# A convolution with max pooling on one core: three row combinations, two loads and the last stores change places

## The chip, the core and the metric

The kernel runs on one core of one Trainium2 chip. Each of the core's engines works through its own list of instructions in order and waits for the others through semaphores: TensorE (PE in the profile) multiplies matrices into PSUM, VectorE (DVE), ScalarE (ACT) and GpSimd (POOL) do elementwise work, and SyncE (SP) issues most of the transfers. GpSimd and ScalarE issue a few transfers too. The metric is the device time of one execution in microseconds. Three runs of the kernel before took 104.82, 105.14 and 105.29 us, so its median is 105.14 us.

## What is computed

```python
# x: 16 images, 64 channels, 64 x 64, fp32;  weight: 128 x 64 x 3 x 3, fp32;  pool_size = 2
x_pad = np.pad(x, ((0, 0), (0, 0), (1, 1), (1, 1)))
conv[b, co] = sum over ci, kh, kw of weight[co, ci, kh, kw] * x_pad[b, ci, kh:kh+64, kw:kw+64]
output[b, co, i, j] = max of conv[b, co, 2*i:2*i+2, 2*j:2*j+2]     # 16 x 128 x 32 x 32
```

## The kernel before

**Tiles.** Two images share the 128 partitions: 64 input channels of the first (half 0) and 64 of the second (half 1). A unit is one quarter of an image pair: 16 rows of the convolution, which after pooling are 8 rows of output. There are 32 units of two kinds, 13 of kind K and 19 of kind W, in the sequence given by `SEQ` (L37). Every matmul uses 64 of the 128 partitions, so a matmul of half 0 and one of half 1 run side by side on PE. The order writes them as pairs, such as `P2.1.0+PBa.1.1`; the first number is the unit, the second the half. A product is three matmuls (the three columns of the 3 x 3 weights), and a pair of products takes PE 0.65 us.

**Fewer products per unit.** For each pair of convolution rows that are pooled together, the kernel does not compute two rows with three weight rows each. It combines input rows (and weight rows) first:

- A W unit has four row combinations, each 128 x 512 and cast to bf16, in `row_op` (L254): `E` or `e` (an odd minus an even row, on VectorE or GpSimd), `S` (their sum, on VectorE), `Z` and `Y` (differences, on GpSimd). Four products use them: `P2` uses E, `P0` uses Z, `P3` uses Y, `P1` uses S.
- A K unit reads a bf16 copy of the input rows for its products `PAa`, `PAb`, `PBa` and `PBb`, and has one row sum, `KS` (VectorE), for its fifth product `PR`.

**From PSUM to the output.** Each unit and half has an even-row bank `ta` and an odd-row bank `tb`, of eight PSUM banks in all. ScalarE copies the even bank to SBUF (`EV`, `ev`: L290). VectorE takes the larger of the even and odd rows, in place (`MX`, `mx`: L299). The product `P1` or `PR` is added after that. ScalarE then copies the odd columns (`OD`, `od`: L303), VectorE takes the larger of the columns (`CM`, `cm`: L327), which frees the bank, and a transfer stores the unit. For a W unit ScalarE also fills the odd bank with the negated even bank (`SE`: L295), once P2 stands there. Capitals before a dot and a number are steps of K units for EV, MX, OD and CM, and small letters those of W units.

**What sets the order.** One list, `ORDER` (L425), gives the order in which instructions are emitted, and with it the order on every engine. Two kinds of waits are added by hand:

- `on_gpsimd` (L81) makes a GpSimd row combination wait for the last VectorE instruction emitted so far that was marked with `on_vector` (the KS, S and E row combinations, and the early weight work and casts).
- `behind` (L73) makes a load wait for a named instruction, kept in `mark`. The input of the W units comes in four chunks for each image pair (`LD.0` to `LD.3` for the first pair, `wload`, L107). LD.1 waits for GM, LD.2 for E.0 and LD.3 for E.1 (L375). All of them are issued by SyncE, which also issues the stores, in order. The input of the K units comes through GpSimd (`L0`, `L1` and so on, `kload`, L101), which issues them in its own order between row combinations.

**The last stores.** The last two units, K 12 and W 18, are stored half by half. `act_left` counts the ScalarE steps that are still to be emitted. While more than one is left, a half is stored by SyncE at once. After that the store is kept in `late` and emitted when no ScalarE step is left, by ScalarE and SyncE in turn.

Of the kernel before, what the change touches and what calls it, by code (L numbers as in the profile page):

```python
# [10 lines left out]
def kernel(  # L11
# [8 lines left out]
    nc = tc.nc  # L20
# [24 lines left out]
    for c in SEQ.lower():  # L45
        i = sum(1 for g in place if g[0] == c)
# [19 lines left out]
    acc = psum.tile([128, 8, R, W], FP32, name="acc")  # L66
# [6 lines left out]
    def behind(inst, other):  # L73
        if other is not None:
            tc.add_manual_dep(inst.ins, other.ins.name, SYNC, reason="order")
# [9 lines left out]
    def rows_of(p, lo, hi):  # L85
        return x[2 * p : 2 * p + 2].rearrange("b c h w -> (b c) h w")[:, lo:hi, :]

    def chunk(q):
        return (2 * R * q + (q > 0), min(H, 2 * R * (q + 1) + 1))
# [17 lines left out]
    def wload(i):  # L107
        loaded.add(i)
        p, q = place["w", i]
        lo, hi = chunk(q)  # L110
        if i % NQ == 0 and q:
            lo -= 2
        return nc.sync.dma_start(
            out=wx[i // NQ % 3][:, lo + 1 : hi + 1, :], in_=rows_of(p, lo, hi)
        )
# [17 lines left out]
    D2, G0, D0, G2, GM, G1, GP = range(1, 29, 4)  # L133
# [48 lines left out]
    ta, tb = {}, {}  # L182
# [69 lines left out]
    mark = {}  # L252
# [33 lines left out]
    ev, od, ot = {}, {}, {}  # L286

    def evac(*g):
        ev[g] = ev_pool.tile([128, R, W], FP32, name="ev")
        nc.scalar.copy(out=ev[g], in_=acc[:, ta[g]])  # L290
        free.add(ta.pop(g))

    def seed(i, h, bank):
# [12 lines left out]
    act_left = [0]  # L306
# [2 lines left out]

    def store_late(dst, src):  # L310
        late.append((dst, src))
        if act_left[0] <= 1:
            flush_late()

    def flush_late():
        while late and act_left[0] == 0:
            stored["late"] = stored.get("late", 0) + 1
            queue = nc.scalar if stored["late"] % 2 else nc.sync
            dst, src = late.pop(0)
            queue.dma_start(out=dst, in_=src)  # L320

    def colmax(c, i, h):
        g = (c, i, h)
        if (c, i) not in ot:
            ot[c, i] = o_pool.tile([128, 2, R, WO], FP32, name="o")
        o = ot[c, i]
        nc.vector.tensor_tensor(  # L327
            out=o[:, h],
            in0=acc[:, tb[g], :, 0::2],
            in1=od.pop(g),  # L330
            op=MAX,
        )
        free.add(tb.pop(g))
        p, q = place[c, i]
        dst = out[2 * p : 2 * p + 2, :, q * R : (q + 1) * R, :].rearrange("b c h w -> c b (h w)")
        src = o.rearrange("p b h w -> p b (h w)")
        stored[c, i] = stored.get((c, i), 0) + 1
        if order_of.index((c, i)) >= len(order_of) - 2:
            if act_left[0] <= 1:
                store_late(dst[:, h], src[:, h])  # L340
            else:
                nc.sync.dma_start(out=dst[:, h], in_=src[:, h])
        elif stored[c, i] == 2:
            nc.sync.dma_start(out=dst, in_=src)
# [27 lines left out]
        return made[0]  # L372

    def load_w(i):
        behind(wload(i), mark.get({0: "D2", 1: "GM", 2: "E0", 3: "E1"}.get(i)))  # L375

    def note(name, inst):
        mark[name] = inst
# [4 lines left out]
    def load_k(n):  # L383
# [22 lines left out]
        "X2": lambda e: cast_more(e, 1, khi2 - klo2),  # L406
        "KX2": lambda: behind(load_second(), mark["D2"]),
        "LD": load_w,
        "L": load_k,
        "KS": lambda i: note(f"KS{i}", ks(i)), "S": ws, "Z": wz, "Y": wy, "SE": seed,  # L410
# [6 lines left out]
    for name, f in ("ev", evac), ("mx", rowmax), ("od", odd), ("cm", colmax):  # L417
        steps[name] = lambda i, h, f=f: f("w", i, h)
        steps[name.upper()] = lambda i, h, f=f: f("k", i, h)
# [4 lines left out]

    ORDER = """  # L425
        D0/V g2 g1/P D2 g0 TD0:1 GS/V TD2:4 KX2 XO1/A TG1:0 VD2/V TG0:2 GP/V XO/A TG2:3 VG0/A
        PAx.0.0:6+PAx.0.1:7 GM/V PAa.0.0+PAa.0.1 VD0/A VG1/V LD.1 PAb.0.0+PAb.0.1 XE/V VG2/A TGM:2 KS.0
        TGP:4 E.0 VGM/A PBa.0.0:0+PBa.0.1:1 EV.0.0 Z.0 VGP/V LD.2 PBb.0.0+PBb.0.1 EV.0.1 MX.0.0
        P2.0.0:4+P2.0.1:3 X1/A S.0 X1b/A L0 PAy.1.0:7+PAy.1.1:2 PAa.1.0+PAa.1.1 SE.0.1:5 MX.0.1 Y.0 SE.0.0:6
        PAb.1.0+PAb.1.1 X2/A E.1 PR.0.0+P0.0.1 EV.1.0 P0.0.0+PR.0.1 EV.1.1 S.1 LD.3 ev.0.1 PBa.1.0:7+P3.0.1 KS.1 Z.1 OD.0.1  # L430
        P2.1.0:2+PBa.1.1:3 OD.0.0 CM.0.1 ev.0.0 mx.0.1 P3.0.0+PBb.1.1 SE.1.0:4 Y.1 PBb.1.0+P2.1.1:1 MX.1.1
        P0.1.0+P1.0.1 CM.0.0 e.2 MX.1.0 SE.1.1:0 P3.1.0+PR.1.1 LD.4 mx.0.0 ev.1.0 PR.1.0+P0.1.1 Y.2 LD.5
        OD.1.1 mx.1.0 od.0.1 P1.0.0+P3.1.1 OD.1.0 CM.1.1 ev.1.1 P1.1.0+P2.2.1:2 cm.0.1 Z.2 od.0.0 mx.1.1
        PAa.2.0:5+PAa.2.1:3 SE.2.1:1 CM.1.0 PAb.2.0+PAb.2.1 L1 od.1.0 cm.0.0 KS.3 PBa.2.0:7+PBa.2.1:6 EV.2.1
        E.3 LD.6 PBb.2.0+P0.2.1 EV.2.0 S.2 LD.7 P2.2.0:3+P1.1.1 KS.2 ev.2.1 Z.3 cm.1.0 PAa.3.0:5+PBb.2.1
# [62 lines left out]
    for s in ORDER.split():  # L498
        act_left[0] -= on_act(s)
        if s[0] == "P":  # L500
            made = []
            for p in s.split("+"):
                p, _, bank = p.partition(":")
                n, i, h = p.split(".")
# [48 lines left out]
```

## Time and profile before

| | |
|---|---|
| Median of 3 runs | 105.14 us |
| The profiled execution, its own time | 105.48 us |
| its span, first to last instruction | 103.6 us |
| PE busy | 97.3 us (94%), 894 matmuls |
| DVE busy | 89.2 us (86%) |
| ACT busy | 81.9 us (79%) |
| POOL busy | 67.1 us (65%) |
| Granted PE clock | 0.995 of full speed |
| DMA moved | 22.81 MB, 220 GB/s on average |

Positions in the text, such as "at 12.50", are microseconds from the start of the span. The profiled execution spends 1.9 us outside its span. PE works with hardly a pause from 16.77 to the end of its list, so what is lost or won before that point shows at the end if the other engines keep up. In the first 17 us PE, DVE and POOL wait for each other and for transfers in turn.

### The profile page before, as it was taken

The numbers are of one execution on the slowest core, as the hardware profiler recorded it, in microseconds if no ns is written. First come the engines' busy times: TensorE is split into PE (matmuls) and PEld (weight loads), VectorE is DVE, ScalarE is ACT, GpSimd is POOL, SyncE is SP. The second block draws the span as 40 slices with busy tenths as digits, with TensorE's granted clock in tenths as the row PEclk, the third lists the DMA queues.
The fourth block names the chain that finished last, engine by engine and source line by source line (L and its number), as shares of the span: only waits on it lengthen the run. The fifth ranks groups of instructions, "written<-read, shape, count | busy, mean of one in ns | idle before, by whom it ended". The sixth has DMA issues, their size and how long they took to land.

```text
span 103.6 us, 2522 instructions
## 1 busy us (share of the span) xinstructions
PE 97.3 (94%) x894; PEld 53.4 (52%) x894; DVE 89.2 (86%) x178; ACT 81.9 (79%) x178; POOL 67.1 (65%) x76
## 2 busy tenths in 40 slices
PE   6899998999999999999999999999999999999920
PEld 2365434555665555555555755555555555666600
DVE  1697598999698999987988999989999999989960
ACT  4579966887897867799879988889889988988640
POOL 7306559947959687976895946892993598590000
PEclk9999999999999999999999999999999999999997
DMA  2987988899999997589989988999956841512352
GB/s 59 354 284 224 234 196 286 237 300 165 284 382 320 161 212 291 192 201 206 218 195 327 357 224 264 299 218 222 378 190 139 197 173 41 196 70 76 131 210 96
DMA packets 13069, 22.81 MB, mean 220 GB/s; under 512 B 1024, under 2 KB 9216, under 8 KB 13056
## 3 DMA queue, kind: packets, MB, share of 16 engines
q1 hardware_dynamic: 12048, 19.63, 58.0%
q0 software_dynamic: 864, 2.88, 18.8%
q8 instruction: 7, 0.11, 0.5%
q10 hardware_dynamic: 144, 0.13, 0.4%
q14 instruction: 6, 0.05, 0.2%
HBM read 17.14 MB, written 8.39 MB: 246 GB/s over the span
## 4 chain that ended last, share of the span: by engine, by line
PE 76%; DMA 8%; DVE 8%; POOL 2%; issue 2%
PE acc L202 75%; DMA wx<-in_x_dram 6%; DMA wraw<-in_weight_dram 3%; DVE acc L299 2%; DVE o L327 2%; POOL wz L260 1%; POOL wy L260 1%; DVE wq L395 1%; DVE we L260 1%; DVE ws L260 1%; DVE wq L364 0%; DVE wq L356 0%; DVE wt L180 0%; PE acc L164 0%; DVE ks L260 0%
## 5 line engine op out<-in xcount | busy, mean ns | idle before, releaser
L202 PEld LDWEIGHTS <-wt 64*128 64x128 bf16 x858 | 50.8, 94 | 41.3 <-issue 1.2
L202 PE MATMUL acc<-kx,wt 64*128 64x512 bf16 (+4 forms) x324 | 57.1, 365 | 0.0
L299 DVE TENSOR_TENSOR acc<-acc,ev 128x512 f32<-128x512 f32 x64 | 42.4, 692 | 4.1 <-PE acc L202 2.5
L290 ACT COPY ev<-acc 128x512 f32<-128x512 f32 x64 | 36.6, 592 | 6.2 <-PE acc L202 5.7
L260 POOL TENSOR_TENSOR wz<-wx 128x512 bf16<-128x512 f32 x19 | 24.1, 1273 | 10.9 <-DVE ks L260 4.6
L202 PE MATMUL acc<-wy,wt 64*128 64x504 bf16 (+1 forms) x114 | 29.6, 377 | 0.4 <-POOL wy L260 0.4
L260 POOL TENSOR_TENSOR wy<-wx 128x512 bf16<-128x512 f32 x19 | 24.1, 1272 | 8.2 <-PE acc L202 3.1
L202 PE MATMUL acc<-wz,wt 64*128 64x504 bf16 (+1 forms) x114 | 29.2, 376 | 0.2 <-POOL wz L260 0.2
L202 PE MATMUL acc<-we,wt 64*128 64x504 bf16 (+1 forms) x114 | 29.1, 377 | 0.0
L202 PE MATMUL acc<-ws,wt 64*128 64x504 bf16 (+1 forms) x114 | 29.1, 377 | 0.0
L327 DVE TENSOR_TENSOR o<-acc,od 128x256 f32<-128x256 f32 x64 | 25.2, 417 | 2.1 <-ACT od L303 1.7
L303 ACT COPY od<-acc 128x256 f32<-128x256 f32 x64 | 23.0, 380 | 4.5 <-PE acc L202 3.7
L295 ACT ACTIVATE acc<-acc 128x512 f32<-128x512 f32 x38 | 22.1, 587 | 3.8 <-DVE o L327 2.1
L202 PE MATMUL acc<-ks,wt 64*128 64x504 bf16 (+1 forms) x78 | 20.2, 377 | 0.0
L260 POOL TENSOR_TENSOR we<-wx 128x512 bf16<-128x512 f32 x11 | 14.0, 1272 | 5.1 <-PE acc L202 3.4
L260 DVE TENSOR_TENSOR ws<-wx 128x512 bf16<-128x512 f32 x19 | 13.9, 738 | 0.0
L260 DVE TENSOR_TENSOR we<-wx 128x512 bf16<-128x512 f32 x8 | 6.0, 750 | 1.1 <-DMA wx<-in_x_dram 1.1
L260 DVE TENSOR_TENSOR ks<-kx 128x512 bf16<-128x512 bf16 x13 | 5.4, 419 | 0.1
L105 POOL DMA_DIRECT2D kx<-in_x_dram x6 | 3.5, 590 | 0.0
L487 PE MATMUL acc<-const-bfloat16-1.0 128*128 128x512 bf16 x6 | 2.7, 623 | 0.8 <-PEq L534 0.8
L356 DVE TENSOR_TENSOR wq<-wraw 128x192 bf16<-128x192 f32 x1 | 0.5, 502 | 2.4 <-DMA wraw<-in_weight_dram 2.4
L164 PE MATMUL acc<-ident,wq 128*128 128x128 bf16 x28 | 2.1, 220 | 0.5 <-DVE wq L395 0.3
(28 smaller groups left out, 17.6 us busy)
## 6 DMA issues: line engine op xcount, KB each, us to landing
out_dram<-o SPq DMA_DIRECT2D x30, 256.0 KB, 4.6
wx<-in_x_dram SPq DMA_DIRECT2D x9, 512.0 KB, 7.1
wx<-in_x_dram SPq DMA_DIRECT2D x5, 480.0 KB, 6.4
wx<-in_x_dram SPq DMA_DIRECT2D x4, 544.0 KB, 6.4
kx<-in_x_dram POOLq DMA_DIRECT2D x3, 496.0 KB, 8.0
kx<-in_x_dram POOLq DMA_DIRECT2D x2, 528.0 KB, 8.9
wx<-in_x_dram SPq DMA_DIRECT2D x1, 576.0 KB, 9.9
ksecond<-in_x_dram SPq DMA_DIRECT2D x2, 256.0 KB, 4.1
```

The costliest lines, as they stand in the source:

```text
L105: return nc.gpsimd.dma_start(out=ktile(i)[:, lo:hi, :], in_=rows_of(p, lo, hi))
L164: nc.tensor.transpose(turned_rows(m)[:, j, :], wq[:, BLOCKS[m] - 1 + j : BLOCKS[m] + 1 + j, :].rearrange("a b c -> a (b c)"), ident,)
L202: lambda kw=kw, o0=o0, o1=o1, c0=c0, c1=c1: nc.tensor.matmul(dst[:, i0:i1, o0:o1], wt[lo : lo + CI, m0 + kw - h, :], rows(lo, i0, i1, c0, c1),
L260: return engine.tensor_tensor(out=r, in0=t[:, f + a : f + a + 2 * R - 1 : 2, :], in1=t[:, f + b : f + b + 2 * R - 1 : 2, :], op=op,)
L290: nc.scalar.copy(out=ev[g], in_=acc[:, ta[g]])
L295: nc.scalar.mul(acc[:, t], acc[:, ta["w", i, h]], -1.0)
L299: nc.vector.tensor_tensor(out=t, in0=t, in1=ev.pop(g), op=MAX)
L303: nc.scalar.copy(out=od[g], in_=acc[:, tb[g], :, 1::2])
L327: nc.vector.tensor_tensor(out=o[:, h], in0=acc[:, tb[g], :, 0::2], in1=od.pop(g), op=MAX,)
L356: inst = engine.tensor_tensor(out=slots(D0), in0=g0, in1=g1, op=SUB)
L395: "D2", on_vector(nc.vector.tensor_sub(out=slots(D2), in0=g2, in1=g1))
L487: warm = nc.tensor.matmul(acc[:, n], src[:, 0:128], src, start=True, stop=True, skip_group_check=True)
```

## The change

- LD.2, the third chunk, is emitted right behind KS.0 and waits for KS.0 where it waited for E.0. The order of SyncE's list stays the same.
- LD.3, the fourth chunk, is emitted behind CM.0.1 and waits for it, where it waited for E.1.
- S.1 leaves its place behind E.1 and is emitted behind MX.1.0, ahead of e.2. KS.1 and Z.1 are emitted directly behind E.1.
- Because `on_gpsimd` looks at the last marked VectorE instruction, e.2 now waits for S.1. It waited for KS.1 before. Z.1 waits for KS.1 as it did.
- The limit for keeping a store in `late` goes from one ScalarE step left to two. So the store of half 0 of W 18 (cm.18.0) is kept as well, and the last three stores go by ScalarE, SyncE and ScalarE. Before, cm.18.0 went by SyncE at once, CM.12.0 by ScalarE and cm.18.1 by SyncE.
- `mark["EV"]` is written and never read.

```diff
     def evac(*g):
         ev[g] = ev_pool.tile([128, R, W], FP32, name="ev")
-        nc.scalar.copy(out=ev[g], in_=acc[:, ta[g]])
+        mark["EV"] = nc.scalar.copy(out=ev[g], in_=acc[:, ta[g]])
...
     def store_late(dst, src):
         late.append((dst, src))
-        if act_left[0] <= 1:
-            flush_late()
+        flush_late()
...
         o = ot[c, i]
-        nc.vector.tensor_tensor(
+        mark["CM"] = nc.vector.tensor_tensor(
             out=o[:, h],
...
-            if act_left[0] <= 1:
+            if act_left[0] <= 2:
                 store_late(dst[:, h], src[:, h])
...
     def load_w(i):
-        behind(wload(i), mark.get({0: "D2", 1: "GM", 2: "E0", 3: "E1"}.get(i)))
+        behind(wload(i), mark.get({0: "D2", 1: "GM", 2: "KS0", 3: "CM"}.get(i)))
...
-        PAx.0.0:6+PAx.0.1:7 GM/V PAa.0.0+PAa.0.1 VD0/A VG1/V LD.1 PAb.0.0+PAb.0.1 XE/V VG2/A TGM:2 KS.0
-        TGP:4 E.0 VGM/A PBa.0.0:0+PBa.0.1:1 EV.0.0 Z.0 VGP/V LD.2 PBb.0.0+PBb.0.1 EV.0.1 MX.0.0
+        PAx.0.0:6+PAx.0.1:7 GM/V PAa.0.0+PAa.0.1 VD0/A VG1/V LD.1 PAb.0.0+PAb.0.1 XE/V VG2/A TGM:2 KS.0 LD.2
+        TGP:4 E.0 VGM/A PBa.0.0:0+PBa.0.1:1 EV.0.0 Z.0 VGP/V PBb.0.0+PBb.0.1 EV.0.1 MX.0.0
         P2.0.0:4+P2.0.1:3 X1/A S.0 X1b/A L0 PAy.1.0:7+PAy.1.1:2 PAa.1.0+PAa.1.1 SE.0.1:5 MX.0.1 Y.0 SE.0.0:6
-        PAb.1.0+PAb.1.1 X2/A E.1 PR.0.0+P0.0.1 EV.1.0 P0.0.0+PR.0.1 EV.1.1 S.1 LD.3 ev.0.1 PBa.1.0:7+P3.0.1 KS.1 Z.1 OD.0.1
-        P2.1.0:2+PBa.1.1:3 OD.0.0 CM.0.1 ev.0.0 mx.0.1 P3.0.0+PBb.1.1 SE.1.0:4 Y.1 PBb.1.0+P2.1.1:1 MX.1.1
-        P0.1.0+P1.0.1 CM.0.0 e.2 MX.1.0 SE.1.1:0 P3.1.0+PR.1.1 LD.4 mx.0.0 ev.1.0 PR.1.0+P0.1.1 Y.2 LD.5
+        PAb.1.0+PAb.1.1 X2/A E.1 PR.0.0+P0.0.1 EV.1.0 P0.0.0+PR.0.1 EV.1.1 KS.1 Z.1 ev.0.1 PBa.1.0:7+P3.0.1 OD.0.1
+        P2.1.0:2+PBa.1.1:3 OD.0.0 CM.0.1 LD.3 ev.0.0 mx.0.1 P3.0.0+PBb.1.1 SE.1.0:4 Y.1 PBb.1.0+P2.1.1:1 MX.1.1
+        P0.1.0+P1.0.1 CM.0.0 MX.1.0 S.1 e.2 SE.1.1:0 P3.1.0+PR.1.1 LD.4 mx.0.0 ev.1.0 PR.1.0+P0.1.1 Y.2 LD.5
         OD.1.1 mx.1.0 od.0.1 P1.0.0+P3.1.1 OD.1.0 CM.1.1 ev.1.1 P1.1.0+P2.2.1:2 cm.0.1 Z.2 od.0.0 mx.1.1
         PAa.2.0:5+PAa.2.1:3 SE.2.1:1 CM.1.0 PAb.2.0+PAb.2.1 L1 od.1.0 cm.0.0 KS.3 PBa.2.0:7+PBa.2.1:6 EV.2.1
         E.3 LD.6 PBb.2.0+P0.2.1 EV.2.0 S.2 LD.7 P2.2.0:3+P1.1.1 KS.2 ev.2.1 Z.3 cm.1.0 PAa.3.0:5+PBb.2.1
```

## The prediction

> **What bounds the kernel now.** I read the busy shares, the chain that ended last, VectorE, GpSimd and PE by time where that chain is not PE, and the issues of transfers. The busy shares and the chain:
>
> ```profile
> PE 97.3 (94%) x894; PEld 53.4 (52%) x894; DVE 89.2 (86%) x178; ACT 81.9 (79%) x178; POOL 67.1 (65%) x76
> ...
> 6.58 5.90 DMA wx<-in_x_dram
> 12.48 0.02 issue
> 12.50 0.69 DVE we L260
> 13.20 0.60 DVE ws L260
> 13.80 0.35 DVE ks L260
> 14.14 0.07 issue
> 14.21 1.27 POOL wz L260
> 15.48 1.24 POOL wy L260
> 16.73 0.04 issue
> 16.77 77.93 PE acc L202 x718
> ```
>
> LD.1, issued at 6.58, lands at 12.48; E.1, S.1 and KS.1 follow on VectorE, Z.1 and Y.1 on GpSimd, and at 16.77 P3.1.0 starts on PE, which then has no pause for 77.93 us. PE's three pauses before that, between starts of pairs that otherwise follow every 0.65 us: 0.17 ahead of P2.1.0 (13.25), 0.33 ahead of P0.1.0 (15.54), 0.58 ahead of P3.1.0. S.1 stands on this chain for 0.60 us though its reader P1.1.0 runs at 18.71. The same stretch and the one behind it, by engine and time:
>
> ```profile
> 13.71 0.42 DVE L260 TENSOR_TENSOR ks<-kx 128x512 bf16<-128x512 bf16 x1
> 14.05 0.42 DVE L327 TENSOR_TENSOR o<-acc,od 128x256 f32<-128x256 f32 x1
> 14.38 1.29 DVE L299 TENSOR_TENSOR acc<-acc,ev 128x512 f32<-128x512 f32 x2
> 15.58 0.41 DVE L327 TENSOR_TENSOR o<-acc,od 128x256 f32<-128x256 f32 x1
> 15.91 1.29 DVE L299 TENSOR_TENSOR acc<-acc,ev 128x512 f32<-128x512 f32 x2
> 17.67 0.70 DVE L299 TENSOR_TENSOR acc<-acc,ev 128x512 f32<-128x512 f32 x1 [0.47 <-ACT ev L290]
> ...
> 16.67 1.28 POOL L260 TENSOR_TENSOR we<-wx 128x512 bf16<-128x512 f32 x1
> 17.90 1.28 POOL L260 TENSOR_TENSOR wy<-wx 128x512 bf16<-128x512 f32 x1
> 19.14 1.27 POOL L260 TENSOR_TENSOR wz<-wx 128x512 bf16<-128x512 f32 x1
> ...
> 20.42 0.42 DVE L260 TENSOR_TENSOR ks<-kx 128x512 bf16<-128x512 bf16 x1
> ```
>
> The last four lines matter most. GpSimd's e.2, Y.2 and Z.2 end at 20.41, and VectorE's KS.3 starts at 20.42. Where a VectorE row combination does start under a GpSimd one, it is stretched:
>
> ```profile
> 77.48 1.19 DVE L260 TENSOR_TENSOR we<-wx 128x512 bf16<-128x512 f32 x1
> ...
> 76.85 1.28 POOL L260 TENSOR_TENSOR wz<-wx 128x512 bf16<-128x512 f32 x1
> ```
>
> The two overlap by 0.64 us and the first takes 0.51 more than its usual 0.68. At 34.72 (1.00 us, overlap 0.45) it is 0.31 more, at 24.77 (0.75, overlap 0.20) 0.06; a KS at 63.31 (0.45 for 0.42) with 0.17 has 0.03. The stretch is the overlap less 0.13: VectorE stands still until 0.13 before GpSimd ends. Column and row maxima, with one operand in PSUM, keep their 0.69 under GpSimd.
>
> **KS.1 and Z.1 directly behind E.1.** KS.1 starts at 13.11, 0.60 earlier. Z.1 runs 13.61 to 14.88 and Y.1 to 16.11. PE can start P0.1.0 at 15.21 (no pause) and P3.1.0 at 16.17: 0.60 earlier than 16.77. This is what the move offers.
>
> **S.1 behind MX.1.0.** VectorE's list is now CM.0.1 (13.45), mx.0.1 (13.78), MX.1.1, CM.0.0, MX.1.0, S.1, mx.0.0, mx.1.0. MX.1.1 needs PBb.1.1, whose last matmul ends at 14.72 as before; with the 0.09 that PE to VectorE takes (17.58 to 17.67) it starts at 14.81. By the steps of the rows above (0.33 for a column maximum, 0.60 for the others): CM.0.0 15.41, MX.1.0 15.74, S.1 16.34 to 17.02, mx.0.0 16.94 to 17.63, mx.1.0 17.54 to 18.24. P1.0.0 waits for mx.0.0 and starts at 17.68 (before 18.06): 0.38 of the 0.60 is left.
>
> **The added wait: e.2 behind S.1.** e.2 starts at 17.10 instead of 16.67. It ends at 18.38, so P2.2.1 starts at 18.43 (before 18.73): 0.30 is left. Queued behind e.2 on GpSimd are Y.2, Z.2 and the load L1. Y.2's reader P3.2.1 is at 23.27, far off. Z.2 ends at 20.83, in time for P0.2.1 at 21.02. L1 is issued 0.43 later, at 20.78.
>
> **Where the rest goes.** VectorE, 0.35 ahead by then, reaches KS.3 at 20.07, under Z.2. By the stretch it ends at 20.83 - 0.13 + 0.42 = 21.12, against 20.84 before. From there to mx.2.1 VectorE has no idle time in the trace (nine instructions, 20.42 to 24.86), so mx.2.1 ends at 25.15 instead of 24.86. P1.2.1 waits for it and starts at 25.20; before it was 25.21. Of the 0.30, 0.01 is left. Behind that VectorE has a gap of 0.61 at 26.46, waiting for ScalarE, which takes up its 0.28; E.5 at 29.36 is stretched by about 0.11, and mx.3.0 then ends 0.15 before P1.3.0 needs it.
>
> The Trainium skill, SBUF — State Buffer, section "Who interferes with whom", says that a Vector instruction with two SBUF inputs contends with a GpSimd instruction that reads SBUF, and that the second to issue blocks until the first has finished. It speaks against this change at KS.3. Blocked to the very end, KS.3 would end at 21.25 and the sum would be 0.13 worse; the measured stretches, all 0.13 short of the overlap, decide.
>
> **LD.2 behind KS.0.** KS.0 ends at 7.81, E.0 at 8.42, so SyncE issues LD.2 at 7.84 instead of 8.45, with nothing else of SyncE's in between. No reader gains: e.2 is its first. The question is LD.1, in flight until 12.48. Bounds from rows: LD.1 takes 5.9 us; the quickest wx load takes 4.9, the median 512 KB one, in fuller queues, 7.1. So -1.0 to +1.2. What it can gain is less: P2.1.0 has a pause of 0.17 only, and MX.1.1, on which S.1 and e.2 hang, moves with PE, so -0.17 at best. I take +0.1: from 9 to 11 us the transfers run at 245 GB/s and other slices reach 382, so there is room for both, and a load that is issued later costs the earlier one little.
>
> The Trainium skill, DMA: Bandwidth & Descriptors, section "Queues, rings and completion order", says that each DMA engine takes a queue's descriptors in ring order. Then LD.2 stands behind LD.1 everywhere, and this term would be about zero.
>
> **LD.3 behind CM.0.1.** CM.0.1 ends at 13.87, so LD.3 is issued at 13.90, not 13.22. With its 5.6 us it lands at 19.5; its first reader E.3 starts at 21.04. Cost nothing; with 7.1 us (21.0) still nothing. SyncE's next entry, the first store, waits for CM.0.0 (15.83), so it is not held up.
>
> **L1.** It took 8.8 us to land, at 29.2. Later by 0.43 it is 29.6; KS.4 reads it at about 30.0 and PAa.5.1 at 30.32. Nothing, or up to 0.3 if LD.3's later bytes push it by 0.68 more (30.3, past KS.4).
>
> **The stores.** SyncE's four last issues stand at 98.68, 99.14, 99.65 and 100.15, ScalarE's at 99.74. cm.18.0 now goes by ScalarE after its last copy (about 99.64), CM.12.0 by SyncE at 99.75, cm.18.1 by ScalarE at 100.10. The last issue moves by -0.05 and the bytes are the same. The trace has only one ScalarE issue; two in a row cost 0.37 each, both before 100.5. I take zero, with -0.05 and +0.37 as ends.
>
> **Sum.** -0.60 offered, +0.22 (mx.0.0), +0.08 (e.2), +0.29 (KS.3 under Z.2), +0.1 (LD.1): +0.09 on the profiled 105.48. That execution is 0.34 above the median of the runs, 105.14, so I forecast 105.14 + 0.09, about 105.2 us.
>
> **Rivals.**
> - *The chain's gain stays whole (faster).* VectorE and GpSimd would have to keep up with PE at P1.0.0, P2.2.1 and P1.2.1. For it: DVE is 86% and POOL 65% busy. Against it: the three starts above. -0.60: 104.54. If only KS.3's stretch fails to appear, -0.30: 104.84.
> - *LD.2 slows LD.1 (the other side).* Everything in the chain hangs on LD.1. If the two share the engines evenly, 0.6 us of company costs up to 0.6 us; at a landing time of 7.1 us it is 1.2. It decides from +0.55 on: 105.7 to 106.3. For it: LD.1 is the one transfer PE waits for. Against it: the spare bandwidth.
> - *L1 comes late.* PAa.5.1 waits on PE from a landing of 30.27 on, 1.1 us later than before; KS.4 from about 29.95. With +0.5 to +0.7 on top: about 105.8.
> - *A quicker LD.1 helps before more than after.* If LD.1 lands early in an execution, before gains all of it and after at most 0.17. With 0.34 between profile and median at stake, 105.3. It lies within the first case.
>
> **Chances.** Within 0.5% (0.53 us, about what a measurement of this kernel can tell from no change): the forecast 0.47 and the partial gain of 0.30, 0.05. Faster: the whole gain, 0.16. Slower: LD.1 late 0.24, L1 late 0.08. The likeliest case alone is 104.9 to 105.6 (from -0.2 to +0.5 around the median); 8 in 10 is 104.55 to 105.9, which leaves out a part of each outer case.
>
> **What would show it.** KS at 13.1, wz at 13.6 and wy ending at 16.1; PE's pause ahead of wy down to about 0.3 (start to start); e.2 at 17.1 waiting for ws; KS.3 at 20.1 taking about 1.0 us instead of 0.42; PE again idle for 0.2 near 25.2, and its unbroken stretch starting there rather than at 16.8. LD.1 landing before 12.4 or after 12.9, a KS.3 of 0.42 us, or a PE pause at 30.3 would prove a step wrong.

## The result: about 1% slower

The changed kernel takes 105.96 us (median of 8 runs, 105.49 to 106.76); the kernel before took 105.10 us beside it (8 runs, 104.79 to 105.33). The ratio is 1.0097, with a 95% interval of 1.0069 to 1.0124: slower, by 0.86 us between the medians. The forecast was 105.2 us, with 105.9 as the upper end of the range.

The execution that was profiled first took 105.49 us, the quickest of the eight, so a second profile of the changed kernel (106.34 us) and a second one of the kernel before (105.20 us) were taken; they are the runs e16 and e12 below.

### The profile page after: what moved, and what is told of

The parts are those of the page before. It is cut to its first block, busy times and chain, and to the rows that moved or that the text cites. A ratio compares the mean times of both kernels' runs of the same rounds, so it can differ in the third digit from the quotient of the medians.

```text
span 103.7 us, 2523 instructions
## 1 busy us (share of the span) xinstructions
PE 97.9 (94%) x894; PEld 60.8 (59%) x894; DVE 90.0 (87%) x178; ACT 81.9 (79%) x178; POOL 67.1 (65%) x76
## 4 chain that ended last, share of the span: by engine, by line
PE 75%; DMA 12%; DVE 4%; POOL 3%; issue 2%
PE acc L202 74%; DMA kx<-in_x_dram 9%; DMA wraw<-in_weight_dram 3%; PE acc L164 2%; DVE o L326 1%; POOL we L260 1%; POOL wz L260 1%; DVE acc L299 1%; DVE wq L394 1%; DVE ws L260 1%; POOL wy L260 0%; DVE wq L355 0%
## 5 line engine op out<-in xcount | busy, mean ns | idle before, releaser
L202 PEld LDWEIGHTS <-wt 64*128 64x128 bf16 x858 | 58.2, 94 | 34.0 <-issue 1.9
L260 DVE TENSOR_TENSOR ks<-kx 128x512 bf16<-128x512 bf16 x13 | 6.1, 468 | 0.6 <-DMA kx<-in_x_dram 0.5
L164 PEld LDWEIGHTS <-wq 128*128 128x128 bf16 x28 | 1.6, 98 | 1.6 <-issue 0.8
```

The source lines that it names most:

```text
L164: nc.tensor.transpose(turned_rows(m)[:, j, :], wq[:, BLOCKS[m] - 1 + j : BLOCKS[m] + 1 + j, :].rearrange("a b c -> a (b c)"), ident,)
L202: lambda kw=kw, o0=o0, o1=o1, c0=c0, c1=c1: nc.tensor.matmul(dst[:, i0:i1, o0:o1], wt[lo : lo + CI, m0 + kw - h, :], rows(lo, i0, i1, c0, c1),
L260: return engine.tensor_tensor(out=r, in0=t[:, f + a : f + a + 2 * R - 1 : 2, :], in1=t[:, f + b : f + b + 2 * R - 1 : 2, :], op=op,)
```

## The profile after

Busy shares and the chain that ended last, from the page of the first profile:

```profile
PE 97.9 (94%) x894; PEld 60.8 (59%) x894; DVE 90.0 (87%) x178; ACT 81.9 (79%) x178; POOL 67.1 (65%) x76
...
PE 75%; DMA 12%; DVE 4%; POOL 3%; issue 2%
PE acc L202 74%; DMA kx<-in_x_dram 9%; DMA wraw<-in_weight_dram 3%; PE acc L164 2%; DVE o L326 1%; POOL we L260 1%; POOL wz L260 1%; DVE acc L299 1%; DVE wq L394 1%; DVE ws L260 1%; POOL wy L260 0%; DVE wq L355 0%
```

The load of the W units (`wx`), which was in the chain before, is gone from it. A load of the K units (`kx`) has come in. The chain in order of time shows which (start, duration, what):

```profile
7.87 8.32 PE acc L202 x80
16.19 0.60 DVE ws L260
16.79 0.07 issue
16.85 1.27 POOL we L260
18.13 0.51 POOL wy L260
18.63 0.68 issue
19.32 1.21 POOL wz L260
20.53 9.82 DMA kx<-in_x_dram
30.35 0.05 issue
30.39 66.65 PE acc L202 x611
```

S.1 ends, e.2 starts (the wait that the change added), Y.2 and Z.2 follow, and behind them GpSimd issues L1 at 20.53. It lands at 30.35, and PE, which used to run without a pause from 16.77 on, now waits for it at 30.39 (PAa.5.1). In the first profile of the kernel before, GpSimd issued L1 here:

```profile
20.35 0.57 POOL L105 DMA_DIRECT2D kx<-in_x_dram  x1
```

It landed at 29.19 there, 1.13 us ahead of PAa.5.1. The prediction named "a PE pause at 30.3" among the signs that a step of it is wrong, and this is that pause. Here are VectorE and GpSimd by time in the same stretch, and then KS.4, which also reads L1's rows (start, duration, engine and line, in brackets the idle time before and what ended it):

```profile
12.15 0.69 DVE L260 TENSOR_TENSOR we<-wx 128x512 bf16<-128x512 f32 x1 [0.87 <-DMA wx<-in_x_dram]
12.76 0.42 DVE L260 TENSOR_TENSOR ks<-kx 128x512 bf16<-128x512 bf16 x1
...
16.10 0.68 DVE L260 TENSOR_TENSOR ws<-wx 128x512 bf16<-128x512 f32 x1
...
19.82 1.05 DVE L260 TENSOR_TENSOR ks<-kx 128x512 bf16<-128x512 bf16 x1
...
30.37 0.43 DVE L260 TENSOR_TENSOR ks<-kx 128x512 bf16<-128x512 bf16 x1 [0.47 <-DMA kx<-in_x_dram]
```

```profile
13.25 1.28 POOL L260 TENSOR_TENSOR wz<-wx 128x512 bf16<-128x512 f32 x1 [1.24 <-DVE ks L260]
14.48 1.27 POOL L260 TENSOR_TENSOR wy<-wx 128x512 bf16<-128x512 f32 x1
16.85 1.27 POOL L260 TENSOR_TENSOR we<-wx 128x512 bf16<-128x512 f32 x1 [1.10 <-DVE ws L260]
...
19.32 1.27 POOL L260 TENSOR_TENSOR wz<-wx 128x512 bf16<-128x512 f32 x1
20.53 0.57 POOL L105 DMA_DIRECT2D kx<-in_x_dram  x1
```

KS.1 and Z.1 stand where the forecast put them behind E.1 (0.61 and 1.10 us after its start). e.2 waits 1.10 us for `ws`. KS.3 takes 1.05 us instead of 0.42. The second profile of the changed kernel has the same chain with a longer wait (chain, then waits between 28 and 34 us):

```profile
20.63 10.49 DMA kx<-in_x_dram
31.11 0.05 issue
31.16 66.65 PE acc L202 x611
```

```profile
PEld L202 <- DMA kx<-in_x_dram: 1.3, 1, 1.3
DVE ks L260 <- DMA kx<-in_x_dram: 1.2, 1, 1.2
PE acc L202 <- DMA kx<-in_x_dram: 0.8, 1, 0.8
```

**One clock for all profiles.** The work ahead of 8 us differs by up to 0.9 us between executions of the same order. So the profiles are laid over each other from the start of TGP, the transposes of block GP, the last of PE's weight work. All numbers are us behind that point, read from the instructions by time; "E.1 ends" and "KS.3" are VectorE's, products are PE's:

| | before, 1st | before, 2nd (e12) | after, 1st | after, 2nd (e16) | order alone (e1) | S.1 early, first form (e9) | S.1 early (e13) | Z.2 out (e15) |
|---|---|---|---|---|---|---|---|---|
| start of TGP | 7.56 | 7.95 | 7.48 | 7.49 | 7.61 | 7.68 | 8.30 | 8.37 |
| LD.1 landed | 4.92 | 3.73 | 4.64 | 4.85 | 4.32 | 4.89 | 3.60 | 3.25 |
| E.1 ends | 5.63 | 5.09 | 5.36 | 5.57 | 5.09 | 5.60 | 5.09 | 5.09 |
| P3.1.0 | 9.21 | 8.66 | 8.33 | 8.53 | 8.12 | 8.95 | 8.44 | 8.12 |
| P1.0.0 | 10.50 | 9.96 | 9.95 | 10.04 | 9.96 | 10.24 | 9.73 | 9.96 |
| L1 issued | 12.79 | 12.25 | 13.05 | 13.14 | 13.04 | 12.53 | 12.01 | 11.82 |
| KS.3 takes | 0.42 | 0.41 | 1.05 | 1.05 | 1.05 | 0.41 | 0.42 | 0.41 |
| P1.2.1 | 17.65 | 17.11 | 17.44 | 17.53 | 17.45 | 17.40 | 16.89 | 17.17 |
| L1 landed | 21.63 | 20.94 | 22.87 | 23.62 | 22.52 | 22.24 | 20.57 | 20.92 |
| PAa.5.1 | 22.76 | 22.22 | 22.91 | 23.67 | 22.57 | 22.50 | 21.99 | 22.28 |
| end | 96.02 | 95.48 | 96.23 | 97.00 | 95.89 | 95.78 | 95.25 | 95.50 |

Against the first profile of before, on which the forecast was built, the change looks nearly harmless (P1.2.1 even 0.21 earlier). Against the second it is 0.33 us late at P1.2.1 and 0.69 to 1.45 at PAa.5.1. In the first profile of before E.1 ends 0.54 us later than in the second, and everything behind it in before's order is 0.54 later too.

## The experiments

Ratios are to the kernel before, run beside each kernel on the same chip, with 95% intervals.

### e1, e2, e3: the three parts alone

```diff
 # e1: order only
-... EV.1.1 S.1 LD.3 ev.0.1 PBa.1.0:7+P3.0.1 KS.1 Z.1 OD.0.1
+... EV.1.1 KS.1 Z.1 LD.3 ev.0.1 PBa.1.0:7+P3.0.1 OD.0.1
-... CM.0.0 e.2 MX.1.0 SE.1.1:0
+... CM.0.0 MX.1.0 S.1 e.2 SE.1.1:0
 # e2: LD.2 behind KS.0 and LD.3 behind CM.0.1 only
 # e3: limit for late stores 2 instead of 1 only
```

> The kernel before with the order of S.1, KS.1 and Z.1 changed alone; LD.2, LD.3 and the last stores as before. Theory L1: in the changed kernel PE waits near 30.4 for L1, the second GpSimd load, because e.2 behind S.1 and the earlier stores and LD.6 of SyncE let L1 start later and in a fuller queue; this part alone makes both, so the time is 105.6 to 106.2 and L1 lands at 29.9 or later. Rival (the chunks LD.2 and LD.3 are to blame, by LD.1 or by the backlog): 104.8 to 105.2, L1 lands at 29.6 or earlier. Rival (the last stores): 104.8 to 105.2.

> The kernel before with LD.2 behind KS.0 and LD.3 behind CM.0.1 alone. Theory L1: L1 is issued at 20.35 as before and lands at about 29.2, so 105.0 to 105.3. Rival (LD.2 slows LD.1): E.1 starts at 13 or later and the time is 105.6 to 106.2. Rival (LD.3's later bytes push L1): E.1 at 12.5, L1 landing past 30, and the same time.

> The kernel before with the last three stores by ScalarE, SyncE, ScalarE alone. Theory L1 and the forecast: 105.0 to 105.2, nothing moves by more than 0.1. Rival (the tail is to blame): 105.6 to 106.0, with more than 5.3 us from the last matmul to the end of the span.

e1: 106.01 us (12 runs), ratio 1.0066 [1.0032, 1.0101]. e2: 105.36 us (12 runs), 1.0016 [0.9989, 1.0044]. e3: 105.09 us (13 runs), 0.9984 [0.9958, 1.0010]. The loss comes with the order of S.1, KS.1 and Z.1. Loads and stores have no effect that these runs can tell. In e2's profile LD.1 landed 5.25 us after its issue; in the two profiles of before it took 5.90 and 4.91.

### e4 to e8: how much of it is L1

```diff
 # e4: changed kernel, L1 ahead of e.2
-... MX.1.0 S.1 e.2 SE.1.1:0      ... PAb.2.0+PAb.2.1 L1 od.1.0
+... MX.1.0 S.1 L1 e.2 SE.1.1:0   ... PAb.2.0+PAb.2.1 od.1.0
 # e5: changed kernel, K 4 to K 7 read the first pair's rows
+    def kread(i):
+        return kx[0] if 4 <= i < 8 else kx[place["k", i][0]]
 # e6: e5, and W 4 to W 7 read the first W buffer
 # e7: kernel before, L1 behind KS.3
+        if n == 1:
+            behind(inst, mark["KS3"])
 # e8: changed kernel, LD.6 and LD.7 behind KS.2
-{0: "D2", 1: "GM", 2: "KS0", 3: "CM"}
+{0: "D2", 1: "GM", 2: "KS0", 3: "CM", 6: "KS2", 7: "KS2"}
```

> The changed kernel with L1 emitted ahead of e.2, in the idle time that GpSimd has there while it waits for S.1, so that it is issued at about 15.8 instead of 20.5. Theory L1: L1 lands before 26, PE has no pause at PAa.5.1, and the time is 104.6 to 105.1; the spread of the runs shrinks from 1.3 us to about 0.5. Rivals (LD.1, the last stores, KS.3 under Z.2): 105.6 to 106.2 as the changed kernel, with the pause elsewhere.

e4: 106.00 us, ratio 1.0063 [1.0032, 1.0093]; the theory's 104.6 to 105.1 was missed. In its profile L1 was issued at 15.66, landed at 24.21, and PE no longer waited at PAa.5.1; that execution took 105.28. But LD.4, issued behind it, then landed at 25.60 instead of 22.26 (first profile of the changed kernel), about when e.4 needs it (25.78), so this run moved the crowding to another load. It decides nothing about the median.

> The changed kernel, in which the K units 4 to 7 read the bf16 rows of the first image pair (tile kx of unit 0) instead of those that the GpSimd loads L1 and L2 bring; both loads are still issued, and nobody waits for them. So the outputs of these four units are left out of the right computation. Theory L1 (PE waits for L1 at PAa.5.1 in most executions): 104.6 to 105.1. Rival (another load of the crowded queue, or the order of VectorE and GpSimd itself): 105.6 to 106.2 as the changed kernel.

> The same, and the W units 4 to 7 also read the rows of the first image pair, so that nobody waits for LD.4 to LD.7 either; these units too are left out of the right computation. All loads are still issued. Theory L1: the same as the kernel without the wait for L1, 104.6 to 105.1. Rival (LD.4 to LD.7 come late in most executions): only this one is down to 104.6 to 105.1. Rival (order of VectorE and GpSimd itself): 105.6 to 106.2.

e5: 105.47 us, ratio 1.0040 [1.0011, 1.0068]: about half of the loss goes when nobody waits for L1, and neither the theory's time nor the rivals' was met. e6: 105.66 us, 1.0035 [0.9999, 1.0072]: LD.4 to LD.7 hold nothing more that these runs can tell. (One of the ten executions of e6 took 582.45 us, for a reason that no profile shows.) In e5's profile P1.2.1 is as late as in the changed kernel (17.45 behind TGP), and at P1.4.0, where VectorE has caught up a part, PE is 0.20 behind the second profile of before (26.21 against 26.01). It loses 0.38 more by the end, most of it in a pause near 66 us, ahead of P1.10.0. That pause is the same stretch once more: VectorE's S.11 takes 1.23 us there instead of 0.81, because GpSimd's Z.12 started at 60.98, 0.60 before S.11, and runs until 62.26 (the overlap of 0.68 less 0.13 is 0.55, on top of its usual 0.68). Z.12 started 0.16 after its load LD.12 landed, 2.6 us later behind TGP than in the second profile of before. This profile is of the slowest of e5's executions (105.93 us); in e4's profile, where PE does not wait for L1 either, 0.20 is lost at P1.4.0 too, and 0.30 at the end.

> The kernel before, with L1 alone moved behind KS.3, so that it is issued at about 20.9 instead of 20.35; nothing else on GpSimd is touched by that, its next step Z.3 waits for KS.2 until 22.4. Theory L1: a load that starts 0.55 later lands 0.5 to 2 later, and the time is 105.4 to 106.2. Rival (L1 has slack, the cause is elsewhere): 104.9 to 105.2.

e7: 107.08 us, ratio 1.0182 [1.0126, 1.0238]. L1 was issued 0.64 us later than in the first profile of before, and the chain of waits shows the whole price in one place:

```profile
19.03 1.23 POOL wz L260
20.27 0.71 issue
20.98 0.02 POOLq L260
20.99 10.87 DMA kx<-in_x_dram
31.86 0.04 issue
31.91 66.65 PE acc L202 x611
```

So L1's place alone is enough to lose 2 us, though by the first profile of before it had a slack of 1.1 us at PAa.5.1 (0.8 at KS.4).

> The changed kernel with LD.6 and LD.7 held behind KS.2, so that SyncE issues them at about 22.4 instead of 20.6 and 21.1, after L1 at 20.5. Theory L1 with crowding (LD.6 and LD.7 take the engines from L1): L1 lands before 29.6 and the time is 104.7 to 105.3. Theory L1 without crowding (its own later issue decides): no better than 105.6 to 106.2.

e8: 105.66 us, ratio 1.0053 [1.0023, 1.0082]. L1, issued at 20.74 and so 13.29 us behind TGP, as late as in the changed kernel, took 8.6 us and landed at 29.30, with no wait ahead of PAa.5.1. The landing is the one that the theory with crowding wanted; the time is not, it is the other theory's. In the changed kernel L1 is issued together with LD.6 (20.53 and 20.55) instead of 0.8 us ahead of it, and that it then shares the engines with LD.6 and LD.7 would explain its late landing; one profile shows it. Half a per cent is left, and the interval overlaps that of the changed kernel. LD.1 landed late in the one profile (P1.0.0 at 10.20 behind TGP), and the other executions of e8 were not profiled, so the runs do not show what this half per cent is made of beside KS.3's stop.

### e9: KS.1 and Z.1 forward, S.1 still early

```diff
 # kernel before
-... EV.1.1 S.1 LD.3 ev.0.1 PBa.1.0:7+P3.0.1 KS.1 Z.1 OD.0.1
+... EV.1.1 KS.1 Z.1 S.1 LD.3 ev.0.1 PBa.1.0:7+P3.0.1 OD.0.1
```

> The kernel before, with KS.1 and Z.1 directly behind E.1 and S.1 behind Z.1: S.1 stays ahead of CM.0.1, so e.2 waits for nothing new. Theory (what costs is S.1's place behind MX.1.0, through e.2, KS.3 and L1): within 0.3% of the kernel before, 104.8 to 105.3 us; e.2 starts at about 16.1, KS.3 takes 0.42 us, L1 is issued no later than in the kernel before, and PE does not wait at PAa.5.1; P1.0.0 stays at about 18.0 since mx.0.0 is as late as before. Rival (bringing Z.1 and all behind it on GpSimd forward is itself the harm): 105.6 us or more.

104.84 us (12 runs), ratio 0.9981 [0.9956, 1.0006]. e.2 started at 16.54, KS.3 took 0.41 us, and PE did not wait for L1. The forecast of the theory holds for the time, KS.3 and PAa.5.1 (e.2 came later than its 16.1): moving KS.1 and Z.1 forward does no harm; S.1's place behind MX.1.0 does.

### e10, e11: nobody waits for LD.1

```diff
-        f = 2 * R * q + pad
+        f = 2 * R * (0 if (name[0], i) == ("w", 1) else q) + pad
```

> The kernel before, where E.1, S.1, Z.1 and Y.1 read the rows of the first W chunk instead of the second, so that nobody waits for LD.1, which is still loaded (the second W unit of the output is wrong). Theory (before follows LD.1): E.1 starts at about 11.3 instead of 12.1 to 12.5, PE's pauses ahead of P2.1.0, P0.1.0 and P3.1.0 go, 104.2 to 104.6 us. Rival (before hangs on the steps behind MX.1.1 as the changed kernel does): less than 0.3 us quicker, 104.8 to 105.1 us.

> The changed kernel with the same edit: E.1, S.1, Z.1 and Y.1 read the rows of the first W chunk, nobody waits for LD.1 (the second W unit of the output is wrong). Theory (after, the early stretch hangs on PBb.1.1, MX.1.1 and S.1, and not on LD.1): at most 0.3 us quicker than the changed kernel, 105.6 to 106.0 us, so the distance to the kernel before with the same edit grows to 1.0 us or more. Rival (both follow LD.1 alike): 105.0 to 105.3 us, distance still 0.9.

e10: 105.13 us, ratio 1.0000 [0.9969, 1.0030]. e11: 106.31 us (4 runs), 1.0109 [1.0061, 1.0158]. The theory was that before gains from an early LD.1 without limit, and it fell: taking LD.1 away from before gives nothing that these runs can tell, and the executions spread as widely without it (104.68 to 105.61). The reason is in the second profile of before, VectorE and then GpSimd by time:

```profile
11.05 0.69 DVE L299 TENSOR_TENSOR acc<-acc,ev 128x512 f32<-128x512 f32 x1
11.71 1.34 DVE L260 TENSOR_TENSOR we<-wx 128x512 bf16<-128x512 f32 x1
12.96 0.68 DVE L260 TENSOR_TENSOR ws<-wx 128x512 bf16<-128x512 f32 x1
```

```profile
11.22 1.27 POOL L260 TENSOR_TENSOR wy<-wx 128x512 bf16<-128x512 f32 x1 [0.56 <-DVE ws L260]
```

LD.1 is there at 11.68 and E.1 starts, but under GpSimd's Y.0, and takes 1.34 us instead of 0.69: the same stretch that the prediction measured elsewhere (overlap 0.78 less 0.13 is 0.65). Y.0 thus sets a floor: E.1 ends 5.09 us behind TGP in e12, e10 (no wait for LD.1 at all), e1, e2, e3, e13 and e15. LD.1 shows only when it lands later than about 4.4 (5.09 less 0.69), and then one for one. In the first profile of before it did, by 0.54.

The changed kernel has a second floor: P1.0.0 starts 9.95 or 9.96 behind TGP in its first profile, in e1 and in e11 (LD.1 landed at 4.64 in the first and at 4.32 in the second; in the third nobody waits for it). That is where before has P1.0.0 too when LD.1 is in time.

### e12: the kernel before again

> The kernel before, unchanged, for a second profile of it. Theory: a span of 103.0 to 103.3 us instead of 103.6, with LD.1 landing at about 12.0 to 12.2 instead of 12.48, and the pause ahead of P3.1.0 shorter by about as much. Rival: the same span with LD.1 where it was, or a shorter one whose difference lies elsewhere (L1, or PE's last stretch).

105.20 us, span 103.4. LD.1 was issued at 6.77 and landed at 11.68, where it had been 6.58 and 12.48. The span is only 0.2 shorter, since TGP started 0.39 later in this execution; behind TGP it is 0.54 shorter. Both the span and LD.1 lie a little outside the forecast, LD.1 on the early side. So in the first profile LD.1 was late, and this one shows the kernel with LD.1 in time. Of the eight profiles in which the loads up to here are those of the kernel before (both of before, e1, e3, e7, e9, e10 and e15) LD.1 landed later than 4.4 behind TGP in three: a late LD.1 is the less common case, not a rare one.

### e13, e14: S.1 back to its early place in the changed kernel

```diff
 # e13: changed kernel
-... KS.1 Z.1 ev.0.1 ...          ... CM.0.0 MX.1.0 S.1 e.2 SE.1.1:0
+... KS.1 Z.1 S.1 ev.0.1 ...      ... CM.0.0 e.2 MX.1.0 SE.1.1:0
 # e14: e13, and LD.6 and LD.7 behind KS.2
```

> The changed kernel with S.1 taken back from behind MX.1.0 to directly behind KS.1 and Z.1, all else as changed. Theory (S.1's place is the whole loss, through e.2's wait, KS.3 under Z.2 and L1): the loss goes, 104.8 to 105.2 us, KS.3 takes 0.42 us, L1 is issued at about 20.1 and PE does not wait at PAa.5.1. Rival (loads, late stores or the earlier Z.1 hold a part of it): 105.4 us or more.

> The one before this, with LD.6 and LD.7 issued behind KS.2, about 1.5 us later, so that L1 shares the engines with less. Theory (L1's landing is what makes single executions of both kernels longer): L1 takes 8.2 to 8.8 us, the median is 104.6 to 104.9 us and the slowest executions are nearer to it. Rival (L1 has enough room once S.1 is early): no difference to the run without the hold, within 0.15 us.

e13: 105.27 us (12 runs), ratio 1.0004 [0.9984, 1.0024]. The loss is gone with this one step; the two loads and the late stores are still as changed. Its VectorE and GpSimd:

```profile
20.40 0.42 DVE L260 TENSOR_TENSOR ks<-kx 128x512 bf16<-128x512 bf16 x1
```

```profile
13.81 1.65 POOL L260 TENSOR_TENSOR wz<-wx 128x512 bf16<-128x512 f32 x1 [0.97 <-DVE ks L260]
15.42 1.27 POOL L260 TENSOR_TENSOR wy<-wx 128x512 bf16<-128x512 f32 x1
16.65 1.27 POOL L260 TENSOR_TENSOR we<-wx 128x512 bf16<-128x512 f32 x1
...
20.31 0.57 POOL L105 DMA_DIRECT2D kx<-in_x_dram  x1
```

e.2 follows Y.1 at once, KS.3 is clear of Z.2, and L1 goes out 12.01 us behind TGP, 1.04 earlier than in the changed kernel. e14: 105.16 us, 1.0000 [0.9978, 1.0023]. L1 took 9.2 us, not the 8.2 to 8.8 that the theory wanted, and the median differs by 0.11: with S.1 early, L1 needs no protection, as the rival had it. Neither e9, e13 nor e14 is faster than the kernel before by more than these runs can tell. In the profiles e13 and e14 end 0.23 us ahead of the second profile of before, counted behind TGP (95.25 against 95.48 for e13); the medians do not show it, and that stays open.

### e15: Z.2 out of KS.3's way

```diff
 # e1's order, Z.2 not emitted
-... cm.0.1 Z.2 od.0.0
+... cm.0.1 od.0.0
-            return taps(a, h, G0, step1(row["wz", i], 0))
+            return taps(a, h, G0, step1(row["wy" if i == 2 else "wz", i], 0))
```

> The kernel before with the new order of S.1, KS.1 and Z.1 alone, and with Z.2 left out (its reader takes Y.2's rows, so the output of the third W unit is wrong). GpSimd then ends at about 19.2 instead of 20.5. Theory (VectorE reaches KS.3 no earlier than before and is stopped there by Z.2, which puts P1.2.1 0.34 us later; L1, queued behind Z.2, does the rest): KS.3 takes 0.42 us, P1.2.1 starts 17.1 us behind the start of GP's transposes instead of 17.45, L1 is issued 1.2 us earlier, 104.8 to 105.2 us. Rival (the place of S.1 costs through mx.0.0 and P1.0.0, not through KS.3): P1.2.1 still at 17.4, 105.5 us or more.

105.03 us (10 runs), ratio 1.0000 [0.9972, 1.0028]. The same order that cost 0.66% costs nothing without Z.2. P1.0.0 is where it was (9.96), so it was not the way of the loss; KS.3 comes out of the stretch and L1 goes out early (20.19):

```profile
20.04 0.75 DVE L327 TENSOR_TENSOR o<-acc,od 128x256 f32<-128x256 f32 x2
20.70 0.41 DVE L260 TENSOR_TENSOR ks<-kx 128x512 bf16<-128x512 bf16 x1
```

VectorE reaches KS.3 12.33 us behind TGP here (20.70 less 8.37), 12.34 in the changed kernel, and 12.32 in the second profile of before: it had won nothing that the stretch could use up. P1.2.1 starts at 17.17 instead of 17.45. KS.3's stop and the late L1 go at once here, so e15 does not say what each of them costs.

### e16: the changed kernel again

> The changed kernel, unchanged, for a second profile, since the first was of its quickest execution. Theory: P1.0.0 starts 9.96 and P1.2.1 17.45 us behind the start of GP's transposes, as in the first profile (or both later by the same, where LD.1 is late), and a wait for L1 ahead of PAa.5.1 of 0.3 to 1.5 us makes up what the time has over 105.2 us. Rival: the time over 105.2 us lies in another stretch, behind PAa.5.1 or ahead of GP's transposes.

106.34 us. Of the 0.77 us that its end lies behind that of the first profile (97.00 and 96.23 behind TGP), 0.09 is there at P1.2.1, through a later LD.1, and 0.76 at PAa.5.1. What this execution has over the quickest one is the wait for L1.

## Why the prediction was wrong, step by step

- **"KS.1 and Z.1 directly behind E.1 ... -0.60": right against the profile it came from, and worth nothing where LD.1 is in time.** P3.1.0 was forecast for 16.17 and came at 15.81, or 8.33 behind TGP against 9.21. But P1.0.0 waits for mx.0.0, two pairs later, and starts at 9.96 in before (second profile) and in the changed order alike. What PE wins at P3.1.0 (0.54, 8.66 to 8.12 in e1) it loses again there.
- **"S.1 behind MX.1.0", "e.2 behind S.1", "KS.3 under Z.2": right as mechanisms.** All came 0.24 to 0.28 us ahead of the forecast (S.1 at 16.10 for 16.34, e.2 at 16.85 for 17.10, KS.3 at 19.82 for 20.07, P1.2.1 at 24.92 for 25.20), because E.1 was 0.35 earlier and MX.1.1, as the prediction has it, "moves with PE". KS.3 took 1.05 us, which is what the stretch gave (21.12 less 20.07). (Of the maxima that keep their time under GpSimd, the prediction's 0.69 is that of row maxima; column maxima take 0.42.) The Trainium skill, SBUF — State Buffer, section "Who interferes with whom", would have VectorE blocked until Z.2 has finished: Z.2 ended at 20.59, and KS.3 ended at 20.87, 0.28 later and less than its own 0.42, so the block ends somewhat earlier here too. e15 shows that what costs comes through Z.2, by KS.3's stop and by L1 queued behind it, and not through mx.0.0.
- **The first step that failed: "That execution is 0.34 above the median of the runs, 105.14, so I forecast 105.14 + 0.09".** A sum made against one execution was carried over to the median as if the 0.34 were the same for both kernels. The profiled execution had LD.1 0.54 us too late, and the change hides just that. In the median of before there is no such delay to hide: with nobody waiting for LD.1 (e10) it is the same to within 0.3%, 105.13 us. The rival "a quicker LD.1 helps before more than after" named this, and gave it 105.3; the profiles show all of the 0.54 as before's gain, and none of it left for the changed order at P1.0.0. By the second profile the terms are -0.54 and +0.54 up to P1.0.0, and +0.34 from KS.3's stop at P1.2.1, of which 0.20 is left at P1.4.0 (e5).
- **The second, and about half of the loss: "L1. ... Nothing, or up to 0.3", a term that was mis-sized.** The same reference hid it. e.2 starts 9.37 behind TGP instead of 8.57 in the second profile of before, so L1 is issued 0.80 later, not 0.43. And the duration of 8.8 us was kept, where it is 9.8 and 10.5 in the two profiles of the changed kernel, in which L1 is issued together with LD.6. The need at about 30.0 and 30.3 was right. L1 landed 1.93 and 2.68 us later behind TGP than in the second profile of before, and PE's wait put PAa.5.1 back by 0.36 and 1.12 against e5, where nobody waits for L1 (22.91 and 23.67 against 22.55; 0.09 of the 1.12 comes from a later LD.1). The rival "L1 comes late", at 105.8 and with a chance of 0.08, named this mechanism. The measured 105.96 also lies in the 105.7 to 106.3 of the rival "LD.2 slows LD.1", whose reason the runs do not bear out.
- **A near hit that is luck.** The sum gave 105.48 + 0.09 for the profiled execution, and the first profile of the changed kernel took 105.49. But that is its quickest execution of eight, and it holds a wait for L1 that the sum put at nothing.
- **LD.2, LD.3 and the stores: right as far as the runs can tell.** e2 and e3 are within the noise, and e13 has all three changes and loses nothing (1.0004, at most 1.0024). The +0.1 for LD.1 is neither shown nor excluded: LD.1 took 5.0 to 6.2 us in the ten profiles with LD.2 behind KS.0 (5.5 on average) and 4.7 to 5.9 in the eight without (5.2).
- **The account.** That the loss comes from S.1's place is shown: the order alone costs 0.66% (e1), it goes when S.1 is early (e13 and e9), and it goes with Z.2 (e15). How it splits is only in part measured. When nobody waits for L1, 0.97% becomes 0.40% by the ratios and 0.86 becomes 0.52 us by the medians (e5). Of what is left, the profiles give 0.20 us to KS.3's stop at P1.4.0; the rest stays open, and the intervals, about 0.3% to each side, are as large as it. No run takes away KS.3's stop and leaves L1 late in the changed kernel; e7 has L1 late without the stop, but in the order of before.

## What to carry to other kernels

Take a second profile before a sum of tenths is made against one: if the part that the change improves happens to be late in that one execution, the change looks better than it is, and its costs look smaller. A load that is issued from the end of a compute engine's list inherits every wait put on that list, so look up which transfers it will then share the engines with, and do not keep its old duration. When an instruction is moved for the sake of one waiting engine, ask whether the next product waits for something that the move makes no earlier.

## What the runs showed of the hardware

- **Issued together with other loads, a load takes longer, and its time varies widely.** L1 (528 KB, issued by GpSimd) took 8.6 to 9.7 us in seven of the eight profiles in which it was issued 11.8 to 12.8 us behind TGP, 0.8 us or more ahead of LD.6, and 11.4 us in the eighth (e3). It took 9.5 to 10.9 us in the seven in which it was issued 13.0 to 13.7 behind TGP, together with LD.6; the averages are 9.3 and 10.2 us. With LD.6 and LD.7 held back it took 8.6 (e8) and, with S.1 early, 9.2 (e14). In e7, against the first profile of before, 0.64 us of later issue became a landing 2.67 us later. While L1 was in flight in the changed kernel (20.6 to 30.3), the transfers that SyncE issues took 67.5% of the DMA engines' time and L1's queue 32.8%; in the second profile of before (20.3 to 28.8) it was 56.6% and 42.7%. The kernel before is exposed to this as well: in the profile of e3, which differs from it only in the last stores, L1 landed at 31.21, and that execution took 106.37 us.
- **The stretch works both ways.** GpSimd's Z.1 took 1.65 us instead of 1.27 when it started under VectorE's S.1 in e13 (13.81, S.1 until 14.33): 0.38, the overlap of 0.52 less 0.14, about what VectorE shows under GpSimd (0.13).
